# Two parts of one kernel rearranged: the rotary halves exchanged by DMA between tiles on the chip, and one more adaLN part in two seams

## The chip, the core and the metric

The kernel is one program on one core of a Trainium2 chip. The metric is the device time of one execution in microseconds (us), as the median of several executions of the same program. Five engines work side by side: TensorE (PE, with its weight loads as PEld), VectorE (DVE), ScalarE (ACT), GpSimd (POOL) and SyncE (SP, which here issues nearly all DMAs). Each engine runs its own list of instructions in a fixed order and waits on semaphores for the others.

## What is computed

The reference runs one stream of 256 rows by 1024 columns through two blocks.

- First block, two layers: a stick-breaking attention, a convolutional feed-forward, a dilated window attention, and again a convolutional feed-forward, each with a norm ahead of it and behind it.
- Second block, two layers, with a context stream beside the x stream: three branches side by side (neighbourhood attention, differential attention with a two-dimensional rotary embedding, a gated MLP), merged, and then a mixture of 16 experts.

Two pieces matter here. The adaLN vector of the second block is one product per layer, and does not depend on the stream, so it can be worked out at any time ahead of its use:

```python
mod = jax.nn.silu(c) @ w_ada[i] + b_ada[i]
sh1, sc1, gt1, sh2, sc2, gt2 = jnp.split(mod[:, None, :], N_MOD, axis=-1)
```

The rotary embedding turns pairs of channels, of which one lies 16 channels behind the other:

```python
def _rot(x, cos, sin):
    x1, x2 = jnp.split(x, 2, axis=-1)
    return jnp.concatenate([x1 * cos - x2 * sin, x1 * sin + x2 * cos], axis=-1)

kb_all = jnp.concatenate([_da_qk(kbc), rope_2d(_da_qk(kb), tabs)], axis=1)
yb = diff_head_norm(diff_attn_blocks(rope_2d(_da_qk(qb), tabs), kb_all, vb_all, lam),
                    da_subln_g[i], lam_init)
```

## The kernel before

All weights come from HBM once, mostly in DMAs of 1 MB, through a ring of buffers (`Ring`, loads at L141 and L148), issued by SP in a fixed order. A load can be issued only when the ring's slot is free again. Each float32 product of the dense parts is made of three products of halves (`mm3`, L86 to L88): a weight `w` is split by ACT into `wh` (L159) and by DVE into `wl` (L161), the activations into `hTh` (ACT, L376) and `hTl` (DVE, L377). The pool of split weights holds two 1 MB weights. A list scheduler lays out the order of every engine once, when the program is built; pools of a few buffers under one tag decide which tile has to wait for which. `weave` puts two lists of units in alternation, so that PE finds projection products between the steps of an attention; `run` takes a list one by one.

**adaLN.** `u_mod` (L486) gives four units for a third of the vector. Each of them loads two `w_ada` blocks of 1 MB and makes 8 products from them into one bank (L509; the profile counts two records for each product). The last unit also runs `fin` (from L513 on): DVE adds the bias tile to the bank (L515, `mt`), PE transposes the sum (L518), and DVE copies it out (L519). In the first layer of the first block, two units ride in the weave of the first attention (`um[:2]`), two come behind its `post_norm` (`um[2:]`); in the first feed-forward, units go in behind chunks 2 and 3 and two behind its `post_norm`. The places behind a `post_norm` are called seams here: there PE has nothing else, because the next layer's norm is still at work on DVE (`xn`, L341), POOL (`rs`, L307) and ACT (L318, L320), after which PE transposes `xn` (L372), and ACT and DVE split it into `hTh` and `hTl`.

**Rotary embedding.** `g_rope` (L1116) projects the keys KB and the queries QB of the differential attention, two halves each, one 128x512 tile `raw` per half, so 4 tiles per layer and 8 in all. ACT brings a half from its bank into `raw` (L1125). `fin` (L1127) multiplies `raw` by a 128x128 matrix `rot` on PE (L1130, two records each), which exchanges the rows in groups of 16 and sets the sign; then DVE takes three operations (L1132 from the bank into `rt`, L1133, L1134). The tiles `raw` and `rt` share the tag "P" with the softmax tiles of the neighbourhood attention, which runs in the same weave: seven buffers (`NP`). The neighbourhood attention's bias tiles `U` come by two DMAs of 96 KB each on SP as well (L1211).

Of the kernel before, what the change touches and what calls it, by code (L numbers as in the profile page):

```python
# [20 lines left out]
S = 256  # L21
# [17 lines left out]
def shape_constants():  # L39
# [10 lines left out]
    ang = np.zeros((128, S), np.float32)  # L50
    rot = np.zeros((128, 128), np.float32)
    for p in range(128):
        axis, half, f = (p % 64) // 32, (p % 32) // 16, p % 16
        pos = (t // GRID_W if axis == 0 else t % GRID_W).astype(np.float32)
        ang[p] = pos * inv[f]
        if half == 0:
            rot[p + 16, p] = -1.0
        else:
            rot[p - 16, p] = 1.0
    rope = np.stack([np.cos(ang), np.sin(ang)], axis=1).astype(np.float32)  # L60
    colmask = np.full((128, 64), NEG, np.float32)
    for p in range(128):
        c = p % 64
        c0 = min(max(c - 8, 0), GRID_W - 16)
        colmask[p, 63 - (c0 + 15):63 - c0 + 1] = 0.0
    return {"c_onehot": onehot, "c_rope": rope, "c_rot": rot, "c_colmask": colmask}


@with_exitstack
def model(ctx, tc, I, out):  # L70
# [203 lines left out]
    def run(*units):  # L274
        weave(*units)
# [287 lines left out]
    def stick_breaking(l):  # L563
        with ExitStack() as st:
# [66 lines left out]
            def av(p):  # L631
                def f():
# [16 lines left out]
            weave(qk(2) + qk(3), [zz(0), zz(1), zz(2), zz(3), lnl(0)])  # L649
            weave(vv(0) + vv(1) + um[:2],  # L650
                  [zz(4), zz(5), zz(6), zz(7), lnl(1), tr(0), tr(1), tr(2), tr(3)])
# [9 lines left out]
            post_norm(np_, acc, gb, xr)  # L661
            run(um[2:])

# [125 lines left out]
    def conv_ffn(l, mid=None):  # L789
        with ExitStack() as st:  # L790
# [48 lines left out]
            for ch in range(1, nch):  # L839
                up(ch)  # L840
                if 1 < ch < (4 if l == 0 else 7):
                    um[ch - 2]()
# [8 lines left out]
            if l == 0:  # L851
                run(um[2:])

# [219 lines left out]
    def attn_streams(l, hp, tail, ring0=None):  # L1073
        win = I["w_in_2"][l]
        with ExitStack() as st0:
# [6 lines left out]
            nc.sync.dma_start(rope, I["c_rope"])  # L1082
            rot = kp.tile([128, 128], F32, name="rot")
            nc.sync.dma_start(rot, I["c_rot"])
            kvc = [kp.tile([128, 4, S], F32, name="kac"), kp.tile([128, 2, 512], F32, name="vac"),
# [30 lines left out]
            def g_rope(parts, h):  # L1116

                out, last = [], None
                for k, col, scale in parts:
                    for i in range(2):  # L1120
                        st = {}

                        def ev(b, st=st, scale=scale):
                            raw = st["raw"] = ap.tile([128, 2, S], F32, name="raw", tag="P", bufs=NP)
                            act.activation(flat(raw), b, AF.Copy, scale=scale)  # L1125

                        def fin(st=st, k=k, i=i):  # L1127
                            raw = st["raw"]
                            b2 = bank("b")
                            pe.matmul(b2, rot, flat(raw), start=True, stop=True)  # L1130
                            t2 = ap.tile([128, 2, S], F32, name="rt", tag="P", bufs=NP)
                            dve.tensor_tensor(t2, two(b2, 256), rope[:, 1:2].to_broadcast([128, 2, S]), op=ALU.mult)  # L1132
                            dve.tensor_tensor(raw, raw, rope[:, 0:1].to_broadcast([128, 2, S]), op=ALU.mult)  # L1133
                            dve.tensor_tensor(k[:, 2 * i:2 * i + 2], raw, t2, op=ALU.add)  # L1134
                        u = u_projT(ring, win[:, col + i * 256:col + i * 256 + 256], h, ev)
                        out += [u[0]] + ([last] if last else []) + [u[1]]
                        last = fin
                return out, last

# [287 lines left out]
            def stream(s, h, start, fill, nxt=None, before_out=None):  # L1427
# [17 lines left out]
                if isx:  # L1445
# [3 lines left out]
                    gv = g_v(vx2, VB, h)  # L1449
                    g2 += [gv[0], turn] + gv[1:]  # L1450
                    ks2, vs2 = [kvc[2], kx2], [kvc[3], vx2]
# [462 lines left out]
```

## Time and profile before

| what | value |
|---|---|
| median of 3 runs | 2504.19 us (2503.9 to 2507.52) |
| profiled execution | 2505.0 us |
| its span, first to last instruction | 2503.3 us |
| PE, DVE, ACT, POOL busy | 94%, 55%, 42%, 5% of the span |
| DMA | 709.11 MB, mean 283 GB/s |
| mean granted TensorE clock | 0.988 of full speed |

The profiled execution is one run: its own time is 0.8 us above the median. Its span leaves out 1.7 us of start and end. Times in the views are microseconds from the start of the span. A row of the timeline gives start, busy time, engine, line, tiles and count, and in brackets the idle time of the engine ahead of it with what ended it. A row of the chain gives start, duration, engine, tile and line: it is followed back from the last instruction, at each step to what released it.

### The profile page before, as it was taken

To read this page: it belongs to the slowest core of one execution; us is meant where nothing else is said; L and a number is where in the kernel's file an instruction comes from. 1 tells how busy PE (TensorE), PEld (TensorE's weight loads), DVE (VectorE), ACT (ScalarE), POOL (GpSimd) and SP (SyncE) were. 2 spreads that over 40 slices of the span, in tenths; PEclk is the share of its full clock that TensorE was granted. 3 is DMA by queue.
4 is the path that set the end of the run, shared out by engine and by line. 5 is a ranking of instruction groups with operands and counts; after the bars stand their busy time and mean duration, and the time that the engine had idled before them with its cause. 6 is when DMAs were issued, how large, how long until landed. Compare 5 with 4: busy or idle time off the path is not lost.

```text
span 2503.3 us, 38427 instructions
## 1 busy us (share of the span) xinstructions
PE 2353.1 (94%) x15004; PEld 1697.7 (68%) x15004; DVE 1386.8 (55%) x2819; ACT 1061.1 (42%) x2152; POOL 129.8 (5%) x188
## 2 busy tenths in 40 slices
PE   8999999999999999999999999998999989877886
PEld 7788979788998998799834433447879963222222
DVE  5687665786866877887711211225688664222223
ACT  5765555565666666565510000006656532000001
POOL 0100000000000100100300000001010000000000
PEclk9999999999999999999999999999999989999999
DMA  7577565577544445746699999996574679999998
GB/s 273 219 253 264 189 219 175 198 264 274 194 142 161 161 161 166 247 141 222 263 387 427 427 426 427 427 411 231 182 234 149 242 288 419 426 427 427 426 427 334
DMA packets 274935, 709.11 MB, mean 283 GB/s; under 512 B 27135, under 2 KB 181489, under 8 KB 220994
## 3 DMA queue, kind: packets, MB, share of 16 engines
q1 hardware_dynamic: 274754, 706.66, 74.3%
q8 instruction: 118, 1.93, 0.3%
q14 instruction: 63, 0.52, 0.1%
HBM read 705.50 MB, written 1.12 MB: 282 GB/s over the span
## 4 chain that ended last, share of the span: by engine, by line
PE 62%; DMA 30%; DVE 5%; ACT 1%; issue 1%; POOL 0%; SPq 0%; DVEq 0%; POOLq 0%; ACTq 0%
DMA w<-in_w_e_dram 29%; PE b L86 14%; PE b L88 13%; PE b L87 13%; PE h L1618 3%; PE acc L86 3%; PE acc L87 3%; PE acc L88 3%; PE b L1202 1%; PE b L509 1%; PE b L1059 1%; DVE wl L161 1%; DMA w<-in_w_ada_dram 1%; PE o L1322 1%; PE b L1261 1%
## 5 line engine op out<-in xcount | busy, mean ns | idle before, releaser
L161 DVE TENSOR_TENSOR wl<-w,wh 128x512 fp32r<-128x512 f32 x896 | 600.9, 696 | 197.7 <-ACT wh L159 159.3
L159 ACT ACTIVATE wh<-w 128x512 fp32r<-128x512 f32 x896 | 530.8, 627 | 226.0 <-PE b L87 113.9
L86 PE MATMUL b<-hTh,wh 128*128 128x256 f32 x1584 | 453.1, 287 | 3.8 <-ACT hTh L386 2.5
L87 PE MATMUL b<-hTl,wh 128*128 128x256 f32 x1584 | 447.7, 283 | 2.4 <-DVE hTl L377 1.3
L88 PE MATMUL b<-hTh,wl 128*128 128x256 f32 x1584 | 448.0, 283 | 0.0
L86 PEld LDWEIGHTS b<-hTh,wh 128*128 128x128 f32 x1584 | 300.2, 190 | 14.7 <-issue 4.4
L87 PEld LDWEIGHTS b<-hTl,wh 128*128 128x128 f32 x1584 | 299.6, 189 | 5.3 <-DVE hTl L377 1.7
L88 PEld LDWEIGHTS b<-hTh,wl 128*128 128x128 f32 x1584 | 300.0, 189 | 0.3 <-DVE wl L161 0.3
L1618 PE MATMUL h<-w,xin 128*64 128x512 f32 x1024 | 255.6, 596 | 1.5 <-DMA w<-in_w_e_dram 1.4
L396 ACT ACTIVATE yh<-yg 128x256 fp32r<-128x256 f32 x96 | 39.2, 417 | 456.2 <-DVE yg L1842 268.0
L1618 PEld LDWEIGHTS h<-w,xin 128*64 128x64 f32 x1024 | 88.7, 136 | 145.1 <-issue 131.8
L1631 PE MATMUL h<-w,xin 128*32 128x512 f32 x512 | 167.4, 624 | 8.0 <-DMA w<-in_w_e_dram 7.1
L1842 DVE SCALAR_TENSOR_TENSOR yg<-y,rg,gt 128x256 f32<-128x256 f32 x64 | 28.1, 477 | 249.5 <-PE y L1811 249.3
L86 PE MATMUL b<-hT,wh 128*128 128x256 f32 x560 | 156.9, 280 | 0.1
L88 PE MATMUL b<-hT,wl 128*128 128x256 f32 x560 | 156.7, 280 | 0.2 <-DVE wl L161 0.2
L87 PE MATMUL b<-hT,wh 128*128 128x256 f32 x560 | 156.5, 280 | 0.0
L1811 PE MATMUL y<-w,hT 128*32 128x512 f32 (+1 forms) x544 | 131.1, 590 | 24.8 <-DMA w<-in_w_e_dram 24.2
L1632 PE MATMUL h<-w,xin 128*32 128x512 f32 x512 | 127.6, 628 | 22.5 <-DMA w<-in_w_e_dram 22.5
L1721 PE MATMUL y<-w,xin 128*64 128x512 f32 x448 | 111.8, 600 | 5.6 <-DMA w<-in_w_e_dram 5.6
L1811 PEld LDWEIGHTS y<-w,hT 128*32 128x32 f32 x544 | 30.6, 112 | 122.4 <-issue 70.3
L88 PEld LDWEIGHTS b<-hT,wl 128*128 128x128 f32 x560 | 105.6, 188 | 0.4 <-DVE wl L161 0.4
L86 PEld LDWEIGHTS b<-hT,wh 128*128 128x128 f32 x560 | 105.5, 188 | 0.3 <-ACT wh L159 0.3
(393 smaller groups left out, 4069.1 us busy)
## 6 DMA issues: line engine op xcount, KB each, us to landing
w<-in_w_e_dram SPq DMA_DIRECT2D x384, 1024.0 KB
w<-in_w_in_dram SPq DMA_DIRECT2D x92, 1024.0 KB
w<-in_w_ada_dram SPq DMA_DIRECT2D x48, 1024.0 KB
w<-in_ffn_w_up_dram SPq DMA_DIRECT2D x44, 1024.0 KB
w<-in_ffn_w_down_dram SPq DMA_DIRECT2D x22, 1024.0 KB
w<-in_dil_w_qkv_dram SPq DMA_DIRECT2D x18, 1024.0 KB
w<-in_w_branch_dram SPq DMA_DIRECT2D x18, 1024.0 KB
w<-in_sb_w_qkv_dram SPq DMA_DIRECT2D x12, 1024.0 KB
```

What stands on the lines that cost most here:

```text
L86: pe.matmul(o, s[0], m[0], start=start, stop=False, skip_group_check=True)
L87: pe.matmul(o, s[0], m[1], start=False, stop=False, skip_group_check=True)
L88: pe.matmul(o, s[1], m[0], start=False, stop=stop, skip_group_check=True)
L159: act.activation(hi, part, AF.Copy)
L161: dve.tensor_tensor(lo, part, hi.bitcast(F32), op=ALU.subtract)
L396: act.activation(hi, src, AF.Copy)
L1618: pe.matmul(hb[2 * j + n][64 * q:64 * q + 64], xin[:, p, k, q].rearrange("p s c -> p (s c)"), ts[j][q][:, kk, n * 512:n * 512 + 512], star ...
L1631: pe.matmul(hb[0][32 * n:32 * n + 32], lhs, t1[:, kk, ns_], **fl)
L1632: pe.matmul(hb[0][64 + 32 * n:96 + 32 * n], lhs, t3[:, kk, ns_], **fl)
L1721: pe.matmul(yb[p][cols.start // 512][64 * q:64 * q + 64, cols.start % 512:(cols.stop - 1) % 512 + 1], xin[:, p, k, :].rearrange("p q s c - ...
L1811: pe.matmul(yb[cols.start // 512][M * q:M * q + M, cols.start % 512:(cols.stop - 1) % 512 + 1], hT[:, k], w, start=kk == 0, stop=last, ski ...
L1842: dve.scalar_tensor_tensor(yg[:, c_], yb[n][:, c_], rg[:, 16 + e:17 + e], gt[:, xs_], op0=ALU.mult, op1=ALU.mult)
```

## The change

- The rotary product on PE, its matrix `rot` and its bank are gone. When ACT has written `raw`, SP copies it into `rt` by 8 DMAs, each of 16 partitions by 512 floats (32 KB), that swap neighbouring groups of 16 partitions; 64 DMAs in all. The sign moves into the sine table. DVE keeps its three operations, with `rt` in place of the bank. `rt` is taken at the evacuation and not in `fin`; `fin` of a half comes after the whole projection of the next half (before: in the middle of it), and the last one after the first two V units.
- One adaLN part leaves the weave of the first attention (`um[:1]` in place of `um[:2]`), one leaves chunk 3 of the first feed-forward. Each of the two seams runs three parts and `fin` in place of two and `fin`. The third place, the second feed-forward of the first block, is as it was.

```diff
-            weave(vv(0) + vv(1) + um[:2],
+            weave(vv(0) + vv(1) + um[:1],
                   [zz(4), zz(5), zz(6), zz(7), lnl(1), tr(0), tr(1), tr(2), tr(3)])
...
             post_norm(np_, acc, gb, xr)
-            run(um[2:])
+            run(um[1:])
...
-                if 1 < ch < (4 if l == 0 else 7):
+                if 1 < ch < (3 if l == 0 else 7):
                     um[ch - 2]()
...
             post_norm(np_, acc, gb, xr)
             if l == 0:
-                run(um[2:])
+                run(um[1:])
...
-                out, last = [], None
+
+                out, fins = [], []
                 for k, col, scale in parts:
                     for i in range(2):
                         st = {}
...
                             raw = st["raw"] = ap.tile([128, 2, S], F32, name="raw", tag="P", bufs=NP)
                             act.activation(flat(raw), b, AF.Copy, scale=scale)
+                            t2 = st["t2"] = ap.tile([128, 2, S], F32, name="rt", tag="P", bufs=NP)
+                            for g in range(4):
+                                for x in range(2):
+                                    to, of = 32 * g + 16 * x, 32 * g + 16 - 16 * x
+                                    nc.sync.dma_start(t2[to:to + 16], raw[of:of + 16])
 
                         def fin(st=st, k=k, i=i):
-                            raw = st["raw"]
-                            b2 = bank("b")
-                            pe.matmul(b2, rot, flat(raw), start=True, stop=True)
-                            t2 = ap.tile([128, 2, S], F32, name="rt", tag="P", bufs=NP)
-                            dve.tensor_tensor(t2, two(b2, 256), rope[:, 1:2].to_broadcast([128, 2, S]), op=ALU.mult)
+                            raw, t2 = st["raw"], st["t2"]
                             dve.tensor_tensor(raw, raw, rope[:, 0:1].to_broadcast([128, 2, S]), op=ALU.mult)
+                            dve.tensor_tensor(t2, t2, rope[:, 1:2].to_broadcast([128, 2, S]), op=ALU.mult)
                             dve.tensor_tensor(k[:, 2 * i:2 * i + 2], raw, t2, op=ALU.add)
-                        u = u_projT(ring, win[:, col + i * 256:col + i * 256 + 256], h, ev)
-                        out += [u[0]] + ([last] if last else []) + [u[1]]
-                        last = fin
-                return out, last
+                        out += u_projT(ring, win[:, col + i * 256:col + i * 256 + 256], h, ev)
+                        if fins:
+                            out.append(fins[-1])
+                        fins.append(fin)
+                return out, fins[-1]
...
-                    g2 += [gv[0], turn] + gv[1:]
+                    g2 += gv[:2] + [turn] + gv[2:]
```

What this does to the order of the engines is seen at three places. Lines behind the change are 2 lower than before it.

DVE in the first seam, behind the first attention, before (`xn` is the next norm's output, `mt` the adaLN sum, `hTl` a half of the next layer's input, `wl` a half of a weight):

```order
L479 TENSOR_TENSOR xn<-acc,gb 128x512 x2
L481 SCALAR_TENSOR_TENSOR xr<-xn,rs,xr 128x512 x2
L341 SCALAR_TENSOR_TENSOR xn<-xr,rs,gb 128x512
L515 TENSOR_TENSOR mt<-mt,b 128x512
L341 SCALAR_TENSOR_TENSOR xn<-xr,rs,gb 128x512 x2
L519 COPY modT_107<-b 128x32
L341 SCALAR_TENSOR_TENSOR xn<-xr,rs,gb 128x512
```

and now:

```order
L477 TENSOR_TENSOR xn<-acc,gb 128x512 x2
L479 SCALAR_TENSOR_TENSOR xr<-xn,rs,xr 128x512 x2
L339 SCALAR_TENSOR_TENSOR xn<-xr,rs,gb 128x512 x4
L513 TENSOR_TENSOR mt<-mt,b 128x512
L159 TENSOR_TENSOR wl<-w,wh 128x512 x2
L517 COPY modT_107<-b 128x32
```

The adaLN sum has moved from behind the first of the four `xn` operations to behind the last. It does the same in the second seam, where it stood behind the second of them.

SP ahead of the second seam, behind the first feed-forward, before (`dil_w_qkv` are the weights of the dilated attention that follows, `gb` a row of gains, `tb` a bias table):

```order
L141 DMA w<-in_ffn_w_down_dram 128x2x1024
L141 DMA w<-in_w_ada_dram 128x2048 x3
L141 DMA w<-in_dil_w_qkv_dram 128x4x512 x2
L141 DMA w<-in_dil_w_qkv_dram 128x8x256
L141 DMA w<-in_dil_w_qkv_dram 128x4x512
L688 DMA tb<-fdist 128x4x256
L470 DMA gb<-in_norm_gains_dram 128x1024
L141 DMA w<-in_dil_w_qkv_dram 128x4x512 x3
```

and now:

```order
L139 DMA w<-in_ffn_w_down_dram 128x2x1024
L139 DMA w<-in_w_ada_dram 128x2048 x5
L686 DMA tb<-fdist 128x4x256
L468 DMA gb<-in_norm_gains_dram 128x1024
L139 DMA w<-in_dil_w_qkv_dram 128x4x512 x6
```

Four weight loads of the next layer, which stood ahead of `tb` and `gb`, now stand behind them, and the `w_ada` loads of the seam's three parts ahead.

SP in the rotary stretch of the second block's first layer, before (`w_in` 128x8x256 are the projection weights of KB and QB, 128x4x512 those of V):

```order
L141 DMA w<-in_w_ada_dram 128x2048 x2
L499 DMA mt<-in_b_ada_dram 2x512 x4
L141 DMA w<-in_w_in_dram 128x8x256
L1211 DMA U<-rpbr 64x6x64 x2
L141 DMA w<-in_w_in_dram 128x8x256
L1211 DMA U<-rpbr 64x6x64 x2
L141 DMA w<-in_w_ada_dram 128x2048 x2
```

and now:

```order
L139 DMA w<-in_w_ada_dram 128x2048 x2
L497 DMA mt<-in_b_ada_dram 2x512 x4
L139 DMA w<-in_w_in_dram 128x8x256
L1127 DMA rt<-raw 16x512 x8
L1211 DMA U<-rpbr 64x6x64
L1127 DMA rt<-raw 16x512 x8
L1211 DMA U<-rpbr 64x6x64
L139 DMA w<-in_w_in_dram 128x8x256
L1211 DMA U<-rpbr 64x6x64 x2
L139 DMA w<-in_w_ada_dram 128x2048
L1127 DMA rt<-raw 16x512 x8
```

The load for the second half of QB, the second `w_in` of each list, now stands behind the exchanges of both halves of KB.

## Rows read from the trace of the kernel before

**Rows 1.** Page, busy tenths in 40 slices of the span, and the chain by engine.
```profile
PE   8999999999999999999999999998999989877886
DMA  7577565577544445746699999996574679999998
PE 62%; DMA 30%; DVE 5%; ACT 1%; issue 1%; POOL 0%; SPq 0%; DVEq 0%; POOLq 0%; ACTq 0%
```

**Rows 2.** Chain, four short windows: start, us, engine, tile, line, records.
```profile
105.99 1.85 PE b L509 x16
...
211.52 1.85 PE b L509 x16
...
1025.80 0.86 PE b L1130 x2
...
1818.88 1.06 PE b L1130 x2
```

**Rows 3.** Timeline of PE, then of DVE, in the first seam.
```profile
143.18 3.64 PE L509 MATMUL b<-w,scT 128*32 128x512 f32 x32
148.38 0.66 PE L518 MATMUL b<-ident,mt 128*128 128x128 f32 x4 [1.56 <-DVE mt L515]
...
152.95 0.39 PE L87 MATMUL b<-hTl,wh 128*128 128x256 f32 x1 [0.62 <-DVE hTl L377]
...
150.21 0.74 DVE L341 SCALAR_TENSOR_TENSOR xn<-xr,rs,gb 128x512 f32<-128x512 f32 x1
```

**Rows 4.** Timeline of PE, DVE, ACT, then SP (from the trace ahead), second seam.
```profile
343.42 3.64 PE L509 MATMUL b<-w,scT 128*32 128x512 f32 x32
349.32 0.74 PE L518 MATMUL b<-ident,mt 128*128 128x128 f32 x4 [2.26 <-DVE mt L515]
349.90 1.91 PE L372 MATMUL b<-ident,xn 128*128 128x128 f32 x16
...
351.88 0.39 PE L87 MATMUL b<-wl,hTh 128*128 128x512 f32 x1
...
349.51 1.41 DVE L341 SCALAR_TENSOR_TENSOR xn<-xr,rs,gb 128x512 f32<-128x512 f32 x2 [0.25 <-POOL rs L307]
...
351.17 2.48 DVE L377 TENSOR_TENSOR hTl<-b,hTh 128x512 fp32r<-128x512 f32 x4
...
350.54 2.07 ACT L376 ACTIVATE hTh<-b 128x512 fp32r<-128x512 f32 x4 [0.61 <-PE b L372]
355.34 2.03 ACT L159 ACTIVATE wh<-w 128x512 fp32r<-128x512 f32 x3 [2.73 <-PE b L88]
...
316.87 19.05 SPq L141 DMA_DIRECT2D w<-in_dil_w_qkv_dram  x4
```

**Rows 5.** Busy time by engine in the two rotary stretches: window, length, PE, PEld, DVE, ACT, POOL.
```profile
985.00:1045.00 60.00, 58.19 (x404) 45.17 (x403) 54.99 (x123) 33.37 (x77) 9.92 (x12) 1.00 0.67 218
1795.00:1845.00 50.00, 48.84 (x346) 37.33 (x345) 44.31 (x89) 28.24 (x64) 7.94 (x10) 1.00 0.65 189
```

**Rows 6.** Timeline of SP's DMA queue in the first rotary stretch.
```profile
992.48 1.16 SPq L499 DMA_DIRECT2D mt<-in_b_ada_dram  x4
...
996.76 0.40 SPq L141 DMA_DIRECT2D w<-in_w_in_dram  x1
997.48 3.91 SPq L1211 DMA_DIRECT2D U<-rpbr  x2
```

**Rows 7.** Timeline of ACT, POOL and PE, and one row of the chain, same stretch.
```profile
1007.60 1.67 ACT L159 ACTIVATE wh<-w 128x512 fp32r<-128x512 f32 x3 [3.61 <-DMA w<-in_w_in_dram]
...
1010.98 0.60 ACT L1125 ACTIVATE raw<-b 128x512 f32<-128x512 f32 x1
...
1012.00 1.00 POOL L1214 TENSOR_TENSOR U<-U,cm 128x384 f32<-128x384 f32 x1 [5.18 <-DMA U<-rpbr]
...
1012.35 1.08 PE L1261 MATMUL b<-pT,s 128*64 128x256 f32 x6 [0.79 <-DVE pT L1252]
...
1004.33 12.71 DMA w<-in_w_ada_dram
```

More of the change, by code (lines that the diff above doesn't have):

```diff
@@ L50, in shape_constants @@
     ang = np.zeros((128, S), np.float32)
-    rot = np.zeros((128, 128), np.float32)
+    sign = np.ones((128, 1), np.float32)
     for p in range(128):
@@ L56, in shape_constants @@
         if half == 0:
[L57 to L60, printed above, removed]
+            sign[p] = -1.0
+    rope = np.stack([np.cos(ang), sign * np.sin(ang)], axis=1).astype(np.float32)
     colmask = np.full((128, 64), NEG, np.float32)
@@ L65, in shape_constants @@
         colmask[p, 63 - (c0 + 15):63 - c0 + 1] = 0.0
-    return {"c_onehot": onehot, "c_rope": rope, "c_rot": rot, "c_colmask": colmask}
+    return {"c_onehot": onehot, "c_rope": rope, "c_colmask": colmask}
 @with_exitstack
@@ L1082, in attn_streams @@
             nc.sync.dma_start(rope, I["c_rope"])
-            rot = kp.tile([128, 128], F32, name="rot")
-            nc.sync.dma_start(rot, I["c_rot"])
             kvc = [kp.tile([128, 4, S], F32, name="kac"), kp.tile([128, 2, 512], F32, name="vac"),
```

## The prediction

> **What bounds the kernel.** I read the page's slices first [rows 1]: PE is busy 9 tenths or more nearly everywhere, and the DMA engines are full only in the two expert stages, near slices 21 to 27 and 34 to 40. The chain says the same: 62% of the span hangs on PE, 30% on DMA. The expert weights are loaded when the attention ahead has let go of its buffers, so a microsecond that PE saves ahead of an expert stage starts that stage's loads earlier and reaches the end. All that the change touches lies ahead of one. The next view is the chain where adaLN parts and rotary products stand [rows 2]; then the timelines of the two seams [rows 3, 4]; then busy times, SP's queue and the waits in the rotary stretches [rows 5 to 7].
>
> A measurement of this kernel can tell about 0.2%, 5.0 us, from no change. The sum is made against the profiled execution, 2505.0 us, 0.8 above the median of the runs.
>
> **The adaLN parts: what leaves.** A part is 8 products, 16 records, and takes 1.85 us of the chain both times where it is to be taken away, at 105.99 in the first attention and at 211.52 in the first feed-forward [rows 2]. Around it PE runs without a gap. That is 2 x 1.85 = 3.7 us less.
>
> **First seam.** PE now does two parts in 3.64 us from 143.18, idles 1.56 us for the bias sum, transposes it (0.66 us) and goes on with the norm; the first product that needs `hTl` starts at 152.95 [rows 3]. A third part would fit into this idle time nearly whole (1.85 against 1.56). But the bias sum on DVE has moved from behind the first norm operation to behind the fourth, as the order shows. The fourth starts at 150.21 and takes 0.74 [rows 3]; less the 0.1 or so of the copy that stood ahead of it, it ends near 150.85, the sum at about 151.5 (I take 0.7 for it, as for a norm operation of the same shape, 1.41 / 2 [rows 4]). PE's order has the four transposes of the sum ahead of the sixteen of `xn`. So these begin near 152.1 in place of 149. From the start of those transposes to the first product with `hTl` I take the pipeline of the second seam: `hTh` follows 0.64 us behind the first transpose (349.90 to 350.54), the first `hTl` follows it by 0.63 us, and each takes 2.48 / 4 = 0.62 us [rows 4]: 152.1 + 0.64 + 0.63 + 3 x 0.62, and the third `hTl`, the one that the product at 152.95 waited for, is there near 155.2. That is 2.3 us later than 152.95; less the 1.85 saved, the seam and its part cost +0.5. Bounds: -1.85 (the part vanishes in the idle time) and +1.5 (all four `hTl` waited for, 0.6 us each, and a little lost on the split).
>
> **Second seam.** Here the next layer's first weights were split long ahead: their loads went out from 316.87 on, and ACT's next split after the seam is only at 355.34 [rows 4]. So PE went straight from transposes to products, and the first with `wl` started at 351.88. After the change the three parts' six `w_ada` loads fill the ring's six slots, and those weights are issued behind the first of these parts, near 345.3. Even landed by 350, ACT's order puts the splits behind the four `hTh`. By steps: the second pair of norm operations ends at 349.51 + 1.41 = 350.9 [rows 4], the sum at 351.6, the sum's transposes by 352.2, `hTh` from 352.85 to 354.9, the first `wh` at 355.5, the first `wl` at 356.3. That is 4.4 us behind 351.88; less 1.85, +2.6. Bounds: -1.85 again, and +4.5 if the load lands 2 us later than that.
>
> Both seams with both parts: **+3.1 us**, from -3.7 to +6.0.
>
> **Rotary products: what leaves.** A product is two records, and the chain counts 0.86 to 1.06 us for one [rows 2]. There are 8: -6.9 to -8.5, and I take **-7.7**. The matrix's load (64 KB, twice) is covered by the other loads. DVE saves nothing, three operations of the same shape before and after.
>
> **Rotary exchange: what comes.** Per half 8 DMAs on SP. The small DMAs of `mt` are issued at 1.16 / 4 = 0.29 us each, and a pair of `U` took 3.91 us where the queue was full [rows 6]: 2.3 to 15.6 us of SP per half. The data of a half, 256 KB, are a quarter of one weight load. Until it has landed: the pair of `U` issued from 997.48 on was used first at 1012.00 [rows 6, 7], some 14 us, which is the high end; the issue alone, 2.3 us, is the low one. I take 6 to 8 us, nearer to `U` at less load, since an exchange shares the DMA engines with 1 MB loads as `U` does. The consumer is `fin`, a whole projection later; the 60 us of the first stretch [rows 5] hold the four halves and the first part of V, some 10 to 12 us each. So it is there in time, with little to spare.
>
> The Trainium skill ("DMA: Bandwidth & Descriptors", Anatomy of one DMA, and Rules for kernel authors) speaks against this: each DMA has a fixed cost of about 2 us, and below 64 KB one pays mostly overhead. An estimate from that page's figures, for eight that run one behind the other, is 8 x 2.1 = 17 us for one half, and by it `fin` would be late each time: the sum would be nearer to the second rival. The trace can't settle it: four DMAs of `mt` are issued within 1.16 us [rows 6], which speaks against a strict row, but no run here shows an exchange.
>
> What queues behind it: SP waits for ACT's `raw` ahead of each exchange, and the weight loads stand behind. The load for QB's second half, issued at 996.76 before [rows 6], now comes behind the exchanges of both halves of KB, at about 1009 us: some 12 us later (`raw` of KB's second half is written at 1010.98 before [rows 7], and some 4 us earlier when ACT no longer stands ahead of it; then SP's 2.3 us). Even at 996.76 it was late for ACT, which stood 3.61 us until 1007.60 for it [rows 7], with softmax work and `raw` behind it in its order, and PE waited 0.79 us for a `pT`. In the changed order that split comes later on ACT, so part of the 12 us is absorbed. DVE is nearly full as well, 54.99 of 60 us and 44.31 of 50 [rows 5], so a wait of DVE for an exchange can't be made up, and PE's 4 us per layer can be passed on only where DVE has these few us to spare. Cost of all this: from 0 (cover holds) to about 6 us per layer (the 3.61 us wait again, on two loads). I take 1.2 per layer, since the rows have idle time on PE to swallow some of it (1.8 us in the first stretch, 1.2 in the second [rows 5]): **+2.4**, from 0 to +12.
>
> **Sum.** +3.1 - 7.7 + 2.4 = -2.2 us: 2505.0 - 2.2 = 2502.8 for the profiled execution, 2502.0 against the median. That is inside what can't be told from no change.
>
> **Rivals.**
>
> *Everything pays.* The exchange hides behind a projection, and the seams swallow the parts in their idle time of 1.56 and 2.26 us [rows 3, 4]. Then -7.7 - 3.7 = -11.4, or with seams at +0.5 in place of -3.7, -7.2: 2493 to 2497. For it: PE is on the chain at the rotary products, with 0.8 to 1.06 us each. Against it: the moved bias sum in both seams, and DVE at 92% of the first stretch.
>
> *The SP queue turns the rotary stretch round.* One mechanism: SP runs in order, so the exchange of a half, waiting for `raw`, holds back the weight load of the half after the next; ACT stands at its split, and PE behind ACT. It decides as soon as that load lands later than PE reaches its projection; from the rows, if an exchange holds SP more than about 6 us: the load issued at 996.76 reached ACT at 1007.60, 10.8 us [rows 6, 7]; with two weights split ahead, 20 to 24 us pass from its turn to its use; so some 11 us are left for the two exchanges ahead of it. One late load costs some 3.6 us as at 1007.60 [rows 7], and with two per layer, 4 x 3.6 = 14.4 us come against -7.7: with the seams at +3.1, +9.8, so 2514; with one per layer, +2.6, 2507. For it: the wait is there already, and `w_ada` loads in this stretch took 12.71 us, a link of the chain [rows 7]. Against it: the split of that weight has moved behind in ACT's order, and four `mt` cost SP 1.16 us only [rows 6].
>
> The rule on small transfers in the Trainium skill ("DMA: Bandwidth & Descriptors", Rules for kernel authors), taken strictly, leads to this rival.
>
> *PE's time doesn't pass.* DVE sets the pace of the rotary stretch, and 4 us less on PE only become waits for DVE; then the rotary part gives -1 or -2 in all and the seams +3.1: 2505 to 2506, no change.
>
> **How the numbers follow.** The forecast 0.34; PE's time doesn't pass, 0.08; the queue rival with one late load per layer, 0.04: these three are within 5.0 us of the median, 0.46 for "same". Everything pays, wholly or with seams at +0.5: 0.31, "faster". The queue rival in its strong form, 0.23, "slower"; I put into it the seams at their upper bound, +6.0, with the exchange at several us per layer, which ends near the same time. The likeliest single case is the forecast, 2502.0. Its own range is 2499 to 2507. The whole range goes from the full gain, 2492, to the queue rival in most of its strength, 2512; about 1 in 10 is left out at either side.
>
> **What would show it.** PE's L1130 and 16 records of L509 in each of the two weaves are gone, and each seam has 48 records of L509. Right: in the first seam the bias sum's transposes start near 151.6 minus the 1.85 us saved ahead, behind about 3 us of idle time on PE in place of 1.56, and in the second seam a new wait for `wh` of 1 to 2 us stands ahead of the first products; measured from the last product of each `acc`, the first `hTl` or `wl` product comes 2.3 and 4.4 us later than before. Right for the rotary part: from the start of the projections to the gates some 3 us less per layer, DVE's wait for `rt` under 1 us each, and the `w_in` load issued near 1009. Wrong: DVE waits of several us on `rt`, ACT waits above 3.6 us on `w_in`, or seams as short as before.

## The result, and the profile after

The changed kernel takes **2546.34 us** (median of 4, 2545.84 to 2546.78), the kernel before on the same chip 2505.31 us (median of 4). The ratio is 1.0162, interval 1.0151 to 1.0174: 41 us slower, where 2502 was forecast, with a range up to 2512. The profiled execution's span is 2544.1 us, against 2503.3.

The page's slices and chain, as [rows 1] (the second row is the granted TensorE clock in tenths of full speed, the last one the chain by line):

```profile
PE   8999999999999999699999999998979989777876
...
PEclk9999999999999999899999999998989999999999
...
PE 60%; DMA 31%; DVE 4%; ACT 2%; SPq 1%; issue 1%; POOL 1%; POOLq 0%; DVEq 0%; ACTq 0%
DMA w<-in_w_e_dram 28%; PE b L84 13%; PE b L86 13%; PE b L85 13%; PE h L1618 3%; PE acc L84 3%; PE acc L85 3%; PE acc L86 3%; DMA U<-rpbr 2%; PE b L1202 1%; DVE wl L159 1%; PE b L1057 1%; PE b L370 1%; PE b L507 1%; SPq L1127 1%
```

Two slices of PE have fallen by more than one tenth: the seventeenth, from 1018 to 1081 us, from 9 to 6, and the thirtieth, from 1844 to 1908 us, from 9 to 7. Two things are new in the chain: the loads of the bias tiles `U` with 2%, some 50 us, and SP's own issue of the exchanges (L1127) with 1%. The first had no place in my sum, and the second only as the delay of one weight load.

Landmarks that both traces share tell where the time came from. Times are from the start of the span:

| landmark | before | after | later by |
|---|---|---|---|
| first `raw` of the second block's first layer | 995.1 | 1000.6 | 5.5 |
| first product of the first expert stage (L1618) | 1254.4 | 1282.3 | 27.9 |
| first `raw` of the second layer | 1802.0 | 1830.2 | 28.2 |
| last product with `vbc` in the differential attention (L1322) | 1939.2 | 1983.2 | 44.0 |
| first product of the second expert stage's last part (L1811) | 2082.1 | 2125.0 | 42.9 |
| end of the span | 2503.3 | 2544.1 | 40.8 |

So the seams and what lies between them give 5.5 us, the two rotary stretches 22.4 and 15.8 us, and the expert stages pass nearly all of it on, giving back some 3.

**The seams.** Timeline of PE after the change, first seam and second seam, for [rows 3, 4]:

```profile
141.00 5.36 PE L507 MATMUL b<-w,scT 128*32 128x512 f32 x48
149.57 0.65 PE L516 MATMUL b<-ident,mt 128*128 128x128 f32 x4 [3.21 <-DVE mt L513]
150.06 3.40 PE L370 MATMUL b<-ident,xn 128*128 128x128 f32 x16
...
342.70 5.36 PE L507 MATMUL b<-w,scT 128*32 128x512 f32 x48
350.86 0.74 PE L516 MATMUL b<-ident,mt 128*128 128x128 f32 x4 [2.80 <-DVE mt L513]
351.44 3.39 PE L370 MATMUL b<-ident,xn 128*128 128x128 f32 x16
356.03 0.73 PE L84 MATMUL b<-wh,hTh 128*128 128x512 f32 x2 [1.21 <-ACT wh L157]
```

Three parts stand in each seam, PE idles 3.21 and 2.80 us for the bias sum, and the second seam has its new wait for `wh`, 1.21 us. These are the steps that the prediction took. One is not: the sixteen transposes of the norm take 3.40 and 3.39 us, against 1.91 [rows 4]. The table by windows (length, then busy time of PE, PEld, DVE, ACT and POOL, then the granted clock, the DMA share and GB/s) tells why:

```profile
149.50:154.00 4.50, 4.41 (x22) 3.97 (x22) 4.14 (x10) 2.34 (x6) 0.53 (x1) 0.62 1.09 385
154.00:160.00 6.00, 5.99 (x50) 5.99 (x51) 5.88 (x10) 4.30 (x10) 0.00 (x0) 1.00 1.06 398
351.00:357.00 6.00, 4.72 (x23) 3.89 (x24) 3.77 (x7) 4.39 (x9) 0.53 (x1) 0.72 1.05 406
```

Behind the idle time the granted clock is 0.62 and 0.72 on the mean, so for part of the window at the lower of its two levels, 1.2 GHz; then it is full again. Before, the granted clock was 1.00 in both seams, with idle times of 1.56 and 2.26 us. The Trainium skill ("TensorE: Matmul & The Clock Gate", Part 1: The HAM clock gate) says that the clock is set by how busy the engine has been of late; these rows agree.

**The rotary stretches.** Busy time in 75 us of each, to be held against [rows 5]:

```profile
990.00:1065.00 75.00, 58.60 (x395) 46.62 (x394) 48.16 (x114) 29.75 (x71) 7.33 (x12) 0.89 0.51 151
1830.00:1905.00 75.00, 59.70 (x372) 44.76 (x371) 53.12 (x111) 34.24 (x82) 9.70 (x12) 0.91 0.56 167
```

PE is busy for 78% of the first and 80% of the second; in [rows 5] it was 97 and 98%. DVE, ACT, POOL and the DMA engines are less busy than before as well: no engine in the stretch is full, so they wait for one another. SP's DMA queue shows the start of it, as [rows 6]:

```profile
1001.19 5.22 SPq L1127 DMA_DIRECT2D rt<-raw  x8
1006.52 0.63 SPq L1211 DMA_DIRECT2D U<-rpbr  x1
1010.29 4.95 SPq L1127 DMA_DIRECT2D rt<-raw  x8
1015.29 0.64 SPq L1211 DMA_DIRECT2D U<-rpbr  x1
1015.97 0.62 SPq L139 DMA_DIRECT2D w<-in_w_in_dram  x1
...
1028.56 4.99 SPq L1127 DMA_DIRECT2D rt<-raw  x8
...
1034.28 1.31 SPq L1211 DMA_DIRECT2D U<-rpbr  x2
```

An exchange holds the queue for 5 us, 0.6 us for each transfer, and can only begin when ACT has written `raw`. SP's waiting holds the queue as well: from 990 to 1085 us it stood 16.5 us in two waits for `raw`. The two transfers of one bias tile, which went out together before, now stand behind two different exchanges: 1006.52 and 1015.29. The chain through the stretch goes round in a circle:

```profile
1015.29 6.67 DMA U<-rpbr
1022.12 1.00 POOL U L1214
1023.14 0.76 DVE b L1230 x2
...
1034.96 10.13 DMA U<-rpbr
1045.25 1.00 POOL U L1214
1046.27 0.76 DVE b L1230 x2
1047.04 0.60 DVE nm L664
1047.66 1.45 ACT P L666 x4
1049.11 2.07 ACT wh L157 x4
1051.18 0.50 ACT raw L1122
1051.69 0.57 SPq L1127
```

The bias tile lands, POOL masks it, DVE adds it to the scores, ACT makes the softmax, then the next weight's split and the next `raw`, which stand behind it in ACT's order; and only this `raw` lets SP issue the next exchange, behind which the next bias tile waits (issued from 1058.13 on). The chain shows this whole round once in each stretch, in the second from the load of `U` at 1857.93 over `raw` at 1874.73 to the next load at 1882.98. At the left-out place, ahead of 1034.96, it runs along DVE's softmax instead; SP's queue, with the exchange begun at 1028.56 in it, had come free only 0.1 us earlier. The exchanges begin at 1010.29, 1028.56 and 1051.69, 18 and 23 us apart; before, one `raw` followed the other by 9 to 16 us. The timelines of DVE and PE show what is late on them:

```profile
1046.27 0.76 DVE L1230 TENSOR_TENSOR b<-b,U 128x256 f32<-128x256 f32 x2 [4.67 <-POOL U L1214]
...
1026.87 0.66 PE L1246 MATMUL b<-ident,P 128*128 128x128 f32 x2 [6.88 <-DVE rc L668]
```

Over the whole kernel DVE waits 27.0 us for `U` (before, 0.9), and for the exchange itself hardly anyone does. ACT's waits for the `w_in` loads, on which the second rival of the prediction rests, have not grown but nearly gone. These are the waits of DVE for POOL's masked `U`, before and after, the one wait for the tile `rt` (of ACT), and ACT's waits for `w_in`, before and after (total, times, longest):

```profile
  POOL U L1214: 0.9, 1
...
  POOL U L1214: 27.0, 9
...
  ACT P L666: 2.5, 1
...
ACT wh L159 <- DMA w<-in_w_in_dram: 16.7, 6, 4.0
...
ACT wh L157 <- DMA w<-in_w_in_dram: 2.6, 1, 2.6
```

### The profile page after: what moved, and what is told of

Same layout as the page of the kernel before. It is cut to its first block, busy times and chain, and to the rows that moved or that the text cites. A ratio compares the mean times of both kernels' runs of the same rounds, so it can differ in the third digit from the quotient of the medians.

```text
span 2544.1 us, 38505 instructions
## 1 busy us (share of the span) xinstructions
PE 2363.3 (93%) x14988; PEld 1706.2 (67%) x14988; DVE 1381.3 (54%) x2819; ACT 1058.9 (42%) x2152; POOL 128.9 (5%) x188
## 4 chain that ended last, share of the span: by engine, by line
PE 60%; DMA 31%; DVE 4%; ACT 2%; SPq 1%; issue 1%; POOL 1%; POOLq 0%; DVEq 0%; ACTq 0%
DMA w<-in_w_e_dram 28%; PE b L84 13%; PE b L86 13%; PE b L85 13%; PE h L1618 3%; PE acc L84 3%; PE acc L85 3%; PE acc L86 3%; DMA U<-rpbr 2%; PE b L1202 1%; DVE wl L159 1%; PE b L1057 1%; PE b L370 1%; PE b L507 1%; SPq L1127 1%
## 5 line engine op out<-in xcount | busy, mean ns | idle before, releaser
L1618 PE MATMUL h<-w,xin 128*64 128x512 f32 x1024 | 256.1, 598 | 1.5 <-DMA w<-in_w_e_dram 1.4
L1618 PEld LDWEIGHTS h<-w,xin 128*64 128x64 f32 x1024 | 89.0, 137 | 145.6 <-issue 132.2
L1811 PE MATMUL y<-w,hT 128*32 128x512 f32 (+1 forms) x544 | 130.2, 586 | 26.0 <-DMA w<-in_w_e_dram 25.1
L1811 PEld LDWEIGHTS y<-w,hT 128*32 128x32 f32 x544 | 29.8, 112 | 123.8 <-issue 69.1
```

The source lines that it names most:

```text
L1618: pe.matmul(hb[2 * j + n][64 * q:64 * q + 64], xin[:, p, k, q].rearrange("p s c -> p (s c)"), ts[j][q][:, kk, n * 512:n * 512 + 512], star ...
L1811: pe.matmul(yb[cols.start // 512][M * q:M * q + M, cols.start % 512:(cols.stop - 1) % 512 + 1], hT[:, k], w, start=kk == 0, stop=last, ski ...
```

## The experiments

Theory: SP issues in order, and eight small transfers per half, which wait for `raw`, delay what stands behind them; and, apart from that, the seams cost some 5 us. Rivals: the exchanged data come too late; the tiles' buffers are held too long; the new places of the rotary units cost the time. "Before" is 2505 to 2506 us in all of these.

### The two halves apart

e1_adaln moves only the adaLN parts, but its edit also hit the seam of the dilated attention, where one part was then done twice.

> The kernel before with only the adaLN parts moved, the rotary product kept. Theory A (the two halves of the change act apart: the seams cost what the aligned products of the two traces show, +5.4 us at 1000 us into the span, most of it in the second seam): 2509 to 2511 us. Rival B (the seams only look late because of the rest of the new order; taken alone they cost the +3.1 us of the prediction or less): 2502 to 2508 us.

Measured: 2513.66 us, ratio 1.0032 (1.0019 to 1.0044). With a part done twice it decides nothing; the edit was made again as e1_adaln2, with the four adaLN lines of the change and nothing else:

```diff
-            weave(vv(0) + vv(1) + um[:2],
+            weave(vv(0) + vv(1) + um[:1],
...
-            run(um[2:])
+            run(um[1:])
...
-                if 1 < ch < (4 if l == 0 else 7):
+                if 1 < ch < (3 if l == 0 else 7):
...
-                run(um[2:])
+                run(um[1:])
```

> The kernel before with only the adaLN parts moved in the two seams, as in the change (in the first try the edit had also hit the dilated attention's seam, where one part was then done twice). Theory A (the halves act apart; the seams cost +5.4 us, of which about 1.5 us per seam are the lower clock that is granted there): 2509 to 2512 us. Rival B (without the rest of the change the seams cost the predicted +3.1 us or less): 2504 to 2508 us.

Measured: **2509.75 us, ratio 1.0018 (1.0008 to 1.0028), +4.6 us.** Theory A's price of 2509 to 2512 holds at its low end. The first seam has the same idle time in this run, and the lower clock again (0.66 from 149 to 154 us). In the second seam the transposes still ran at the full clock, but a few microseconds later, behind a further wait of 1.35 us for `wh`, it fell there too, and the products took 0.63 us in place of 0.39. The last row is that stretch in the table by windows, with a granted clock of 0.51:

```profile
149.68 1.12 PE L518 MATMUL b<-ident,mt 128*128 128x128 f32 x4 [3.21 <-DVE mt L515]
150.59 2.95 PE L372 MATMUL b<-ident,xn 128*128 128x128 f32 x16
...
351.60 0.74 PE L518 MATMUL b<-ident,mt 128*128 128x128 f32 x4 [2.80 <-DVE mt L515]
352.19 1.91 PE L372 MATMUL b<-ident,xn 128*128 128x128 f32 x16
...
358.16 0.63 PE L86 MATMUL b<-wh,hTh 128*128 128x512 f32 x1
...
358.00:361.00 3.00, 3.00 (x8) 2.32 (x8) 2.75 (x5) 1.03 (x2) 0.00 (x0) 0.51 1.05 408
```

So the clock is one part of it, and it fell in both seams, in the change and in this run. Where it fell on the transposes, they took some 1.5 us more; in the second seam of this run eight products did (3.3 us from 357.40 on, where eight take 1.9 at the full clock).

e2_exch is the other half: the changed kernel with these four lines put back.

> The kernel before with only the rotary exchange, adaLN parts where they were. Theory A (the exchange is the loss: +21 us in the first rotary stretch, +16 us in the second by the aligned products): 2538 to 2543 us. Rival B (the loss needs both halves, since moved adaLN loads change what the rings hold in the rotary stretch): under 2530 us.

Measured: **2544.07 us, ratio 1.0154 (1.0137 to 1.0171), +38 us.** The exchange is the loss, and the halves add up to about the whole (38.1 + 4.6 against 41.0).

### Who issues

e3_exch_act and e4_exch_pool are e2_exch with one word changed:

```diff
-                                    nc.sync.dma_start(t2[to:to + 16], raw[of:of + 16])
+                                    nc.scalar.dma_start(t2[to:to + 16], raw[of:of + 16])
```

> The exchange alone, but its 8 DMAs per half are issued by ACT, which writes the tile they copy, and no longer by SP. Theory A (what costs is the order of SP's queue: it waits for the tile and then issues for 5 us, and bias tiles and weight loads stand behind): most of the loss goes, 2500 to 2512 us; the 5 us of issue per half now lie on ACT, which has idle time there. Rival B (the exchanges' data come too late for DVE, or the tiles' buffers are held too long: not a matter of who issues): 2530 us or more.

Measured: 2532.52 us, ratio 1.0113 (1.0096 to 1.0129). **A miss:** 12 of the 38 us went, not most of them, and the time is in rival B's range. But it is not B's reason that the trace shows: DVE waited for the exchange for 2.8 us in the whole run. The timeline of ACT tells what took the place of SP's delay:

```profile
1008.85 8.42 ACTq L1127 DMA_DIRECT2D rt<-raw  x8
1017.31 0.69 ACT L666 ACTIVATE P<-b,nm 128x512 f32<-128x512 f32 x1 [8.19 <-DMA rt<-raw]
```

ACT is held for 8.42 us by one exchange, longer than SP was, and its softmax work stands behind. In the traces the transfers of SP and ACT tell of their landing by the same eight semaphores in turn (those of GpSimd use eight others), and each waits for the landing of the one that used its semaphore before it. So ACT, in the middle of this exchange, stood 0.9 us for a load of `U` and 2.6 us for a 1 MB load, both issued by SP. Over the run the softmax on ACT waited 47.5 us for the exchange. The wait had moved from SP to ACT, which has the softmax behind it.

For e4_exch_pool the word is `gpsimd`.

> The exchange alone, issued by GpSimd, whose transfers do not share the eight completion counters that SP's and ACT's do. Theory A (the loss comes from eight small transfers in SP's queue: 5 us of issue, the wait for the tile, and every eighth transfer waited for, 1 MB loads among them): nearly all of the loss goes, 2500 to 2512 us. Rival B (the exchanged data come too late, whoever issues them, or the new order of the projections costs the time): 2525 us or more.

Measured: 2515.94 us, ratio 1.0044 (1.0028 to 1.0061), between the two prices: most of the loss goes, not nearly all. POOL's transfers land without SP's queue, but late for the rotation. In one stretch, waits of DVE and PE (total, count, longest):

```profile
DVE raw L1131 <- DMA rt<-raw: 15.1, 2, 11.1
...
PE b L1261 <- DVE pT L1252: 11.4, 1, 11.4
```

Here the exchange's own time, the first rival, does show: DVE stands up to 11.1 us for it, and PE behind DVE.

### Buffers

e5_u3 is e2_exch with a third buffer for `U` (`bufs=3` at L1209).

> The exchange alone on SP, with three buffers in place of two for the bias tiles U, so that they can be loaded a head earlier. Theory A1 (the bias tiles are what comes late behind the exchanges): half of the loss or more goes, 2510 to 2525 us. Theory A2 (the weight loads are what comes late, the bias tiles are hidden behind them): under 5 us of it go, 2535 us or more. Rival B (buffers of the tiles raw and rt, or the exchange's own time): 2538 us or more as well.

Measured: 2538.26 us, ratio 1.0136 (1.0119 to 1.0153): 6 of the 38 us go, a time that theory A2 (2535 us or more) and rival B (2538 or more) both allow, and not A1. But it decides nothing: with the third buffer the scheduler put the two loads of the next `U` behind two and three exchanges in SP's order in the first stretch, and not ahead of them, so the run did not do what it was made for, and says little of `U`.

e10_poolnp8 is e4_exch_pool with `NP = 8`, e11_np8 the order test below with the same.

> The exchange issued by GpSimd, with eight buffers under that tag. Theory A (its +10.7 us are what the new places cost and, above all, DVE's waits of up to 11 us for transfers that land behind 1 MB loads, buffers play no part): 2512 to 2518 us. Rival B (buffers): 2508 us or less.

Measured: 2517.94 us, ratio 1.0046 (1.0031 to 1.0062), as with seven buffers. The buffers of the tag play no part there.

### The order alone

e8_order keeps the product and moves the rotary units to the places that they have in the change:

```diff
-                        u = u_projT(ring, win[:, col + i * 256:col + i * 256 + 256], h, ev)
-                        out += [u[0]] + ([last] if last else []) + [u[1]]
+                        out += u_projT(ring, win[:, col + i * 256:col + i * 256 + 256], h, ev)
+                        if last:
+                            out.append(last)
                         last = fin
...
-                    g2 += [gv[0], turn] + gv[1:]
+                    g2 += gv[:2] + [turn] + gv[2:]
```

> The product on PE kept, but the rotary units at the places that they have in the change: a half's rotation behind the whole projection of the next half, the last one behind two V units. Theory A (only the transfers cost): 2500 to 2509 us, as before. Rival B (the new places themselves make the softmax and the projections wait for each other): 2515 us or more.

Measured: 2511.13 us, ratio 1.0023 (1.0013 to 1.0032). Between the two prices: the places cost about 5.9 us, without any transfer. With eight buffers, and with only the first of the two edits:

> The rotary product at the places that it has in the change, with eight buffers in place of seven under the tag that raw, rt and the softmax tiles share. Theory A (the +6 us of those places come from raw being held a projection longer, so that softmax tiles wait for a buffer): 2504 to 2508 us. Rival B (they come from the order itself: DVE's three operations now stand ahead of softmax work): 2510 us or more.

Measured: 2512.07 us, ratio 1.0026 (1.0017 to 1.0035): not the buffers.

> The product kept, the rotation of a half behind the whole projection of the next half, but the last rotation at its old place behind one V unit. Theory A (the later rotation of each half costs the 6 us): 2509 to 2513 us. Rival B (the place of the last rotation does): 2503 to 2508 us.

Measured: 2507.91 us, ratio 1.0015 (1.0006 to 1.0024). The median lies at the upper end of rival B's price, but the interval reaches into theory A's. By the medians each edit has a share of some 3 us; that the second edit has one is not clear of the noise. In the first stretch of e8_order PE waits for DVE's copy of a transposed softmax tile:

```profile
PE b L1262 <- DVE pT L1253: 3.1, 2, 1.7
```

Before, this wait was 0.8 us once [rows 7]. It is the same 3.1 us in e17_fins, so it belongs to the first edit. That DVE's three operations of a rotation now stand ahead of such copies would explain it; I have not shown it by a run that moves those three alone.

### The number of transfers

e9_two64 replaces the eight transfers by two of 64 partitions. They bring the same bytes to the same tile, but exchange rows at a distance of 64 and not of 16.

```diff
-                            for g in range(4):
-                                for x in range(2):
-                                    to, of = 32 * g + 16 * x, 32 * g + 16 - 16 * x
-                                    nc.sync.dma_start(t2[to:to + 16], raw[of:of + 16])
+                            for x in range(2):
+                                nc.sync.dma_start(t2[64 * x:64 * x + 64], raw[64 - 64 * x:128 - 64 * x])
```

> The exchange alone on SP, but of two transfers of 64 partitions per half in place of eight of 16: the same bytes to the same tile, and not the rotary partner (rows are exchanged at a distance of 64). Theory A1 (it is the number of transfers: issue time and places among the eight counters): most of the loss goes, 2500 to 2515 us. Theory A2 (it is SP's wait for the tile, whatever is issued behind it): 2525 us or more.

Measured: **2513.53 us, ratio 1.0038 (1.0024 to 1.0052)**: 30 of the 38 us go. What is left, 8 us, is little more than the order alone. But the scheduler also set SP's list anew (the load of QB's second half came ahead of KB's second exchange), so the next two runs leave out everything but the transfers. They are the kernel before, product and places as they were, with transfers from `raw` into a tile that nobody reads, eight or two per half:

```diff
                             act.activation(flat(raw), b, AF.Copy, scale=scale)
+                            xt = ap.tile([128, 2, S], F32, name="xt", tag="xt", bufs=1)
+                            for g in range(4):
+                                for x in range(2):
+                                    to, of = 32 * g + 16 * x, 32 * g + 16 - 16 * x
+                                    nc.sync.dma_start(xt[to:to + 16], raw[of:of + 16])
```

> The kernel before, product kept, and eight transfers of 32 KB per half from raw into a tile that nobody reads. Theory A (the transfers in SP's queue are the loss, since bias tiles and weight loads wait behind them): 2520 us or more. Rival B (the queue alone is harmless; the loss needs the new places, or something that waits for the data): 2505 to 2512 us.

Measured: **2542.21 us, ratio 1.0152 (1.0137 to 1.0168), +37 us.** Nobody waits for these data, and the whole loss is there. In SP's list of this run the two transfers of each `U` stand together, and the load for QB's second half ahead of KB's second exchange, so the loss doesn't hang on those places. The waits for `U` in this run, the first of POOL for the load, the second of DVE for POOL:

```profile
  DMA U<-rpbr: 91.3, 11
  POOL U L1219: 24.5, 8
```

> The same with two transfers of 128 KB per half. Theory A1 (the number of transfers counts): 2505 to 2510 us, well below the run with eight. Theory A2 (SP's wait for raw counts, whatever stands behind it): within 5 us of the run with eight.

Measured: 2519.48 us, ratio 1.0058 (1.0042 to 1.0073), +14 us, and DVE's wait for `U` is small again:

```profile
  POOL U L1217: 2.5, 1
```

So the number counts for some 23 us, and two transfers that wait for `raw` in SP's queue still cost 14. That is above theory A1's 2510: SP's wait itself, or the place that the scheduler gives the loads behind it, has a share. The unread tile has one buffer only, and this may have a share as well: SP waited 6.5 us for the transfers into it of the half before (1.3 us in e15_idle8), and DVE 2.6 us until `raw` had been read.

### The seam, mended

e13_late leaves three parts in each seam, but the bias sum and its transposes follow the first units of the next stage; e14_late2 does the same with the two parts of the kernel before.

```diff
             post_norm(np_, acc, gb, xr)
-            run(um[1:])
+            run(um[1:4])
+            later.append(um[4])
...
             up(0)
+            if l == 0:
+                later.pop()()
```

> The adaLN parts in the seams as in the change (three parts, rotary product kept), but the bias sum and its transposes come only behind the first units of the next stage. Theory A (a seam is late because the sum stands behind the fourth norm operation on DVE and its transposes ahead of the norm's on PE, so that PE idles 3 us): nearly all of the +4.6 us of the adaLN change goes, 2502 to 2506 us; in the first seam the norm's transposes follow the third part with less than 1 us of idle time. Rival B (the weights of the next stage, loaded late behind six adaLN loads, set the seam's end): 2508 us or more, with the wait for wh of the second seam as long as before.

Measured: 2507.7 us, ratio 1.0007 (0.9998 to 1.0016): by the medians about half of the +4.6 goes; the interval allows anything from nearly none to all of it. The timeline of PE, first and second seam, and the second seam's products in the table by windows:

```profile
148.14 1.32 PE L372 MATMUL b<-ident,xn 128*128 128x128 f32 x8 [0.92 <-DVE xn L341]
...
347.38 1.32 PE L372 MATMUL b<-ident,xn 128*128 128x128 f32 x8 [0.52 <-DVE xn L341]
351.20 1.22 PE L86 MATMUL b<-wh,hTh 128*128 128x512 f32 x2 [2.50 <-ACT wh L159]
...
352.00:355.00 3.00, 3.00 (x10) 2.41 (x10) 3.00 (x7) 2.69 (x6) 0.53 (x1) 0.50 1.05 409
```

Theory A is right for the idle time ahead of the transposes, 0.92 and 0.52 in place of 3.21 and 2.80 us. Theory B is right for the second seam's end: the wait for `wh` has grown from 1.35 (e1_adaln2) to 2.50 us, since the weights come no earlier. Behind it PE runs at the lower clock, 0.50 from 352 to 355 us, while the first seam stays at 1.00. So the second seam keeps its price, the wait and the clock.

> The kernel before, its two adaLN parts per seam where they were, but the sum and its transposes behind the first units of the next stage. Theory A: PE's idle time of 1.56 and 2.26 us ahead of the transposes shrinks, some 1 us per seam: 2502 to 2504 us. Rival B (the norm itself ends no earlier): 2505 us, as before.

Measured: 2504.56 us against 2505.44, ratio 0.9998 (0.9988 to 1.0008): no difference that can be told. No version beat the kernel before.

## Why the prediction was wrong, point by point

- **Seams, +3.1 predicted, +4.6 measured** alone (interval of the ratio 1.0008 to 1.0028, so 2 to 7 us). The steps were right: the sum behind the fourth norm operation, 3 us of idle time, the wait for `wh` in the second seam, 1.2 us where 1 to 2 was said. Left out was what idle time does to the granted clock: 0.62 and 0.72 behind it, and 1.5 us more for the same transposes. From each seam's start to the first product with `hTl` or `wl` it took 3.2 and 5.7 us longer than before, where 2.3 and 4.4 were said. The term was mis-sized, and the lower clock, which no step of it had, is enough to explain by how much.
- **Parts removed from the weaves, -3.7**: e1_adaln2 contains it, it was not run by itself. With the first part gone the first seam begins at 141.00 in place of 143.18, about 2 us earlier; the second begins at 342.70 in place of 343.42, with the first seam's loss in it.
- **Rotary products, -7.7**: no run shows this term by itself. The kernel with idle transfers and the product (2542.21) is as slow as the exchange without it (2544.07), but the second also has the new places of the rotary units, which cost 5.9 us alone and can hide a saving of about that size. That PE's 1 us per half is idle time elsewhere as long as SP's circle sets the pace is argued, not shown.
- **Rotary exchange, +2.4, range 0 to +12: this step failed.** It measured +22 and +16 us by the landmarks, +38 for e2_exch, both with the saved products and the new places in them. Transfers that nobody reads cost 37 us by themselves (e15_idle8): SP's queue was the loss, not the data. The issue lay within its range (2.3 to 15.6 us per half, 5 measured), but the working went on with the low end, 2.3; what made the pair of `U` take 3.91 us in [rows 6] the rows don't show. The place was in the second rival, in-order SP queue and `raw` ahead of it, but with the wrong victim and a price per event in place of a price per turn. I asked what a late weight load costs on ACT, 3.6 us. That load went out at 1015.97, which without the 5.5 us of the seams is near the 1009 that I had said; but ACT's waits for `w_in` fell from 16.7 us to 2.6. And I left out the loads of `U`, which stand between the exchanges in the very order that I showed for SP, and whose user POOL already waited 5.18 us in [rows 7]. Behind exchanges of 5 us each they come late, and DVE's scores with them (4.67 us at 1046.27). Last, I treated each lateness as an event that ends; but `raw` itself stands behind the softmax in ACT's order, so the next exchange starts later too.
- **The order of the rotary units, taken at nothing: it costs about 5.9 us** (e8_order). The prediction moved the rotations one projection back and named no work behind them on DVE.
- **Full DVE as the bound (third rival)**: no. DVE was busy 48.16 and 53.12 of 75 us after the change, less than before.
- **The rule of the Trainium skill** ("DMA: Bandwidth & Descriptors", Rules for kernel authors) that transfers under 64 KB are mostly overhead pointed the right way, and I put it aside because four small loads were issued in 1.16 us. The fixed cost of 2 us that I took from the Trainium skill ("DMA: Bandwidth & Descriptors", Anatomy of one DMA) is given there for transfers that GpSimd issues. Eight such transfers strictly one behind the other the trace does not show, since SP issued them 0.6 us apart. Eight of 32 KB cost 37 us and two of 128 KB 14 us with the same bytes (e15_idle8, e16_idle2). By these runs it is not the engines' time that is lost, the DMA share fell, but the queue's.
- **The passing on to the end** was right: 43 us at the second expert stage, 41 at the end.

What stays open: that `U` is the load whose lateness costs most is read from the waits and the chain, since e5_u3, made to test it, did not; how the 14 us of e16_idle2 divide between SP's wait for `raw`, the one buffer of the unread tile and the new places of the loads in SP's list; and which of DVE's operations makes the 5.9 us of the order. An exchange by fewer transfers that is also the right one was not tried.

## What to carry to other kernels

A transfer that waits for a tile puts its wait into the queue of the engine that issues it: before a product is replaced by transfers, list what stands behind them in that queue, small loads too, and who waits for each. Ask for every lateness whether it returns to its own start: here the tile that the transfer waits for stood behind the work that the delayed load feeds, so that the delay came again with a later half. And idle time of PE in a seam has two prices, its length and the lower clock behind it.

## What the runs showed of the hardware that was not expected

- An issue of a 32 KB transfer between two tiles takes SP 0.59 us (median of 64), twice the 0.29 us of the small loads of `mt` and about as long as a 96 KB load of `U` (0.62, median of 32, before). On ACT it takes 0.60 us, and eight of them 8.42 us, waits included.
- The granted clock was 1.00 behind idle times of 1.56 and 2.26 us, and fell behind 3.21 and 2.80 us, to a mean of 0.62 and 0.72 in windows of 4.5 and 6 us. In e1_adaln2 it was still 1.00 right behind the same 2.80 us and fell some 6 us later, to 0.51; in e13_late it was 0.50 behind 2.50 us. In the rotary stretches, with PE busy 78 to 80%, the mean was 0.89 and 0.91.
- Transfers issued by POOL took 484 ns each on POOL (median of 64), and DVE waited for them up to 11.1 us, while 1 MB loads were under way.
